# HGRN scores as pairs of 64-column products in the two column halves of the PE array

## The chip, the core and the metric

One Trainium2 chip; the kernel runs on one of its cores. The engines named below are TensorE (PE, with its weight loads as a track of their own, PEld), VectorE (DVE), ScalarE (ACT), GpSimd (POOL) and SyncE (SP, which issues DMAs). The metric is the device time of one execution in microseconds (us), lower is better.

## The reference

One layer of a decoder trunk over 1024 tokens of 1024 features: a normed input projection feeds three mixers (HGRN2, a dilated-window attention, RWKV-7), whose outputs are projected and added to the input; a gated MLP with a short convolution, a gated embedding and a last norm follow. All inputs and outputs are float32. What matters here is HGRN2, with 4 heads of 128 keys and 128 values:

```python
def hgrn2_mix(q_raw, f_raw, i_raw, g_raw, lower_bound, gnorm_g):
    q = jax.nn.silu(q_raw.astype(f32))
    f = lower_bound + (1.0 - lower_bound) * jax.nn.sigmoid(f_raw.astype(f32))
    k = 1.0 - f
...
    def step(state, inp):
        qc, kc, vc, lfc = inp
        b = jnp.cumsum(lfc, axis=2)
        b_last = b[:, :, -1:, :]
        o_inter = jnp.einsum('bhck,bhkv->bhcv', qc * jnp.exp(b), state)
        rel = jnp.where(causal[:, :, None], b[:, :, :, None, :] - b[:, :, None, :, :], -jnp.inf)
        scores = jnp.einsum('bhik,bhjk,bhijk->bhij', qc, kc, jnp.exp(rel))
        o_intra = jnp.einsum('bhij,bhjv->bhiv', scores, vc)
        state = (jnp.exp(b_last[:, :, 0, :])[..., None] * state
                 + jnp.einsum('bhck,bhcv->bhkv', kc * jnp.exp(b_last - b), vc))
        return state, o_inter + o_intra
```

A score of query i and key j is their product over the 128 keys, each weighted by the product of the forget gates between j and i.

## The kernel before, in words

The kernel works in stages. `phase_mix` (line 324) runs the norm, the RWKV-7 mixer together with most of the input projections, and then, interleaved, the four HGRN heads, the window attention and what is left of the projections. `phase_out` projects the mixers' outputs, and the FFN (`phase_up`, `phase_down`) and the embedding follow. All data lie as 128 features by 1024 tokens. Large products are split into three products of rounded float32 parts (`mm3`, line 134).

An HGRN head (`hgrn_head`, line 839) is a Python generator. It takes the sequence in 8 chunks of 128 tokens, held in an order in which the first half of a tile runs backwards; 4 chunks are in each half. Scores of a chunk are a 128 by 128 square, keys by queries, and are built up by levels. The own scores (distance 0, lines 867 to 872) come first: for both halves i, four matmuls of a 128 by 128 key block with a 128 by 128 query block into the PSUM tile `sc`, and a copy through a mask, `copy_predicated`, which writes into S only where the mask is set. Then level l = 1 to 7 (lines 886 to 906) handles pairs of neighbouring blocks of n = 2^(l-1) tokens: keys of one block, queries of the other. `keys(l)` (line 878) gathers the keys on ACT into `ks`; four matmuls (line 891) make `sc`, of which line 893 copies what `mask(l)` selects into S3[0], the first half of S. Lines 894 to 896 multiply gates into one half of the keys `k` (on POOL for odd l, on DVE for even) and of the queries `qt` (on DVE), and line 901 combines the gates of neighbouring blocks for the next level. After level 7 the first half S3[0] holds scores of both sequence halves, and lines 907 and 908 part them: what lies above the diagonal (`mask(8)`) is copied to S3[1] and then set to zero in S3[0]. S3[1] was cleared beforehand by POOL (line 858).

Of every 128 by 128 score square, levels 1 to 6 and the own scores use only the two 64 by 64 squares on the diagonal, level 7 only the two off it. The rest of the product is computed and masked away.

After the levels, values and keys are transposed on PE (`vt`, lines 914 and 920), chunk states are formed (`hkv`, line 935; `hst`, 944) and the outputs follow from scores and states (`hpo`, lines 954 and 956).

The masks are ten 128-column tables in `cst` (lines 54 to 58), loaded once by `load_masks` (line 302) and cast to bytes by POOL; `hgmask(l)` (line 307) picks one.

PSUM: HGRN, the attention and the late projections share four one-bank tiles, tag "mx". The attention uses two tiles of two banks, tag "dp". Around the change work the attention's scores (`swq`, line 1035, 64 rows of the array by 128 columns), its transposes (`swt`, line 1058), its outputs (`swo`, line 1071: 128 rows, 64 columns, one head in each column half) and the projections `zp` (lines 139 to 143 by way of `project_late`).

Two things set the order. `phase_mix` interleaves the generators by a list written out by hand (lines 341 to 344): A is heads 0 and 2, B heads 1 and 3, each handing over after 14 steps, C the attention, F and M projections. From what is so traced, a planner in the build sets the order of instructions on each engine by its own costs of the instructions, and the space of tiles; an engine then executes its queue in that order.

Of the kernel before, what the change touches and what calls it, by code (L numbers as in the profile page):

```python
# [10 lines left out]
F32 = mybir.dt.float32  # L11
# [7 lines left out]
P = 128  # L19
T = 1024  # L20
HT = 512
# [15 lines left out]

CC_ID, CC_BONE, CC_MSK, CC_I64 = 0, 128, 256, 384
NC0 = CC_HG = 448
NCC = CC_HG + 10 * 128  # L40


def shape_constants():
    c = np.zeros((P, NCC), np.float32)
    pp = np.arange(P)[:, None]
    ff = np.arange(P)[None, :]
    c[:, CC_ID:CC_ID + P] = pp == ff
    same = (pp // 64) == (ff // 64)
    c[:, CC_BONE:CC_BONE + P] = same
    f64 = np.arange(64)[None, :]  # L50
    c[:, CC_MSK:CC_MSK + 64] = pp % 64 < f64
    c[:, CC_MSK + 64:CC_MSK + 128] = pp % 64 <= f64
    c[:, CC_I64:CC_I64 + 64] = pp % 64 == f64
    c[:, CC_HG:CC_HG + P] = pp == ff
    for l in range(7):
        n = 1 << l
        c[:, CC_HG + (l + 1) * P:CC_HG + (l + 2) * P] = (pp // n) ^ 1 == ff // n
    c[:, CC_HG + 8 * P:CC_HG + 9 * P] = pp < ff
    u = np.arange(T)[None, :]
    d = pp - (u - 896)  # L60
    cnt = ((d >= 0) & (d <= 128)).astype(np.float64)
    cnt += (d >= 0) & (d <= 512) & (d % 4 == 0)
    cnt += (d >= 0) & (d <= 2048) & (d % 16 == 0)
    sw = np.where(cnt > 0, 8.0 * np.log(np.maximum(cnt, 1.0)), -1e30).astype(np.float32)
    return c, sw
# [26 lines left out]
class Trunk:  # L92
# [183 lines left out]
    def setup(self):  # L276
# [7 lines left out]
        self.id64 = self.cst[:, CC_I64:CC_I64 + 64]  # L284
        self.cmask = cp.tile([P, NCC - NC0], U8, name="cmask")
        few = cp.tile([P, 8], F32, name="few")
# [15 lines left out]
    def load_masks(self, tp):  # L302
        t = tp.tile([P, NCC - NC0], F32, name="ctmp")
        self.nc.gpsimd.dma_start(t, self.a["cst"][:, NC0:])
        self.nc.gpsimd.tensor_copy(self.cmask, t)

    def hgmask(self, l):
        o = CC_HG - NC0 + l * P
        return self.cmask[:, o:o + P]


    def proj(self, j):
# [526 lines left out]
    def hgrn_head(self, h):  # L839
        nc, mxp, par, spool = self.nc, self.mxp, self.par, self.spool  # L840
        j0 = 8 + 4 * h

        def view(t, off, *dims):
            return bass.AP(t.tensor, t.offset + off, [t.ap[0], *dims])

        f = self.zload(j0, self.slot)
        q = self.zload(j0 + 1, self.slot)
        yield
        nc.vector.tensor_scalar(f, f, self.olb[:, h:h + 1], self.lb[:, h:h + 1], ALU.mult, ALU.add)
        k = self.slot("hk")  # L850
        for a, b in ((0, HT), (HT, 0)):
            nc.vector.tensor_scalar(k[:, a:a + HT], f[:, b:b + HT], -1.0, 1.0, ALU.mult, ALU.add)
        qt = self.slot("qt")
# [1 line left out]
        yield  # L855

        S = self.slot("hS")
        nc.gpsimd.memset(S[:, HT:], 0.0)
        S3 = [S[:, a:a + HT].rearrange("p (c i) -> p c i", i=P) for a in (0, HT)]

        def mask(l):
            return self.hgmask(l).unsqueeze(1).broadcast_to([P, 4, P])

        Tt = self.slot("hT")
        off = 0
        Tc = f
        for i in (0, 1):
            sc = mxp.tile([P, 4, P], F32, tag="mx", name=self.nm("hsc"))
            for c in range(4):
                nc.tensor.matmul(sc[:, c, :], k[:, (1 - i) * HT + c * P:(1 - i) * HT + (c + 1) * P],  # L870
                                 q[:, i * HT + c * P:i * HT + (c + 1) * P], start=True, stop=True)
            nc.vector.copy_predicated(S3[i], mask(0), sc)

        def blocks(l):
            n = 1 << (l - 1)
            return n, HT // n, ([HT + n, 2], [2 * n, 256 // n], [1, n])

        def keys(l):
            n, nb, half = blocks(l)
            ks = spool.tile([P, HT], F32, tag="sqt", name=self.nm("ks"), bufs=2)  # L880
            nc.scalar.copy(view(ks, 0, [n, 2], [2 * n, nb // 2], [1, n]), view(k, 0, *half))
            return ks

        ks = keys(1)
        yield
        for l in range(1, 8):
            n, nb, half = blocks(l)
            qq = view(qt, 0, *half)
            sc = mxp.tile([P, 4, P], F32, tag="mx", name=self.nm("hsc"))
            for c in range(4):  # L890
                nc.tensor.matmul(sc[:, c, :], ks[:, c * P:(c + 1) * P],
                                 view(qt, c * P, [2 * n, 64 // n], [HT + n, 2], [1, n]), start=True, stop=True)
            nc.vector.copy_predicated(S3[0], mask(l), sc)
            (nc.gpsimd if l % 2 else nc.vector).tensor_tensor(
                view(k, 0, *half), view(k, 0, *half), view(Tc, nb + 1, [-nb - 1, 2], [2, nb // 2], [0, n]), ALU.mult)
            nc.vector.tensor_tensor(qq, qq, view(Tc, 1, [nb - 1, 2], [2, nb // 2], [0, n]), ALU.mult)
            if l < 7:
                ks = keys(l + 1)
            Tn = Tt[:, off:off + nb]
            T3 = Tc.rearrange("p (b two) -> p b two", two=2)  # L900
            nc.vector.tensor_tensor(Tn, T3[:, :, 0], T3[:, :, 1], ALU.mult)
            Tc = Tn
            off += nb
            if l == 7:
                vc = self.zload(j0 + 2, self.slot)
            yield
        nc.vector.copy_predicated(S3[1], mask(8), S3[0])
        nc.vector.copy_predicated(S3[0], mask(8), self.zero.unsqueeze(1).broadcast_to([P, 4, P]))

        V = self.slot("hV")  # L910
        for hf in (0, 1):
            pt = mxp.tile([P, HT], F32, tag="mx", name=self.nm("vt"))
# [35 lines left out]
        o = self.slot("ho")  # L948
# [710 lines left out]
def lay_out(inp):  # L1659
    f = {k: np.asarray(v) for k, v in inp.items()}  # L1660

    def cols(v):
        return v.reshape(-1, P).T

    lora = np.concatenate([f["rwkv_w2"][0], f["rwkv_a2"][0]], axis=0)
    par = np.concatenate(
        [cols(f["norm_mix_g"][0]), cols(f["norm_ffn_g"][0]), cols(f["norm_ple_g"][0]), cols(f["final_norm_g"]),
         cols(f["hgrn_lower_bounds"][0]), cols(f["hgrn_gnorm_g"][0]), cols(f["rwkv_mu"][0]),
         cols(f["rwkv_w0"][0]), cols(f["rwkv_a0"][0]), cols(f["rwkv_k_k"][0]), cols(f["rwkv_k_a"][0]),
         cols(f["rwkv_r_k"][0].reshape(-1)), cols(f["rwkv_ln_w"][0]), cols(f["rwkv_ln_b"][0]),  # L1670
         cols(f["ffn_conv_w"][0].reshape(-1)), cols(f["ffn_conv_b"][0]), lora, f["rwkv_g2"][0]], axis=1)
    cst, swm = shape_constants()
    return {
        "xT": np.ascontiguousarray(f["x"][0].T).reshape(ND, P, T),
        "pT": np.ascontiguousarray(f["p"][0, 0].T).reshape(2, P, T),
        "w_in": col_blocks(f["w_in"][0], in_blocks()),
        "w_out": col_blocks(f["w_out"][0], range(0, 1024, P)),
        "ffn_up": col_blocks(f["ffn_up"][0], range(0, 5632, P)),
        "ffn_down": np.ascontiguousarray(f["ffn_down"][0]).reshape(NFF, P, 1024),
        "ple_gate": col_blocks(f["ple_gate"][0], range(0, 1024, P)),  # L1680
        "ple_proj": np.ascontiguousarray(f["ple_proj"][0]).reshape(2, P, 1024),
        "par": np.ascontiguousarray(par),
        "cst": cst,
        "swm": swm,
    }
# [17 lines left out]
```

## Time and profile before

| | us |
|---|---|
| median of 3 runs | 1486.92 (1485.7 to 1489.24) |
| profiled execution, its own time | 1488.94 |
| its span | 1487.2 |
| mean granted PE clock | 0.99 |
| HGRN and attention stage, about | 425 to 640 |

A page of the profile tells one execution: busy time of each engine, forty slices of the span, the DMA queues, the chain of work that ended last, and the costliest groups of instructions. Besides the page, the trace answers questions on stretches of time, groups by line and shape, waits and single instructions. L891 is line 891 of the kernel. `128*64 128x128 x8` in a PE row are array rows by array columns used, the moving operand and the count. A float32 matmul stands as two instructions, its two passes. `x28: 684/736/755` are least, median and largest duration in nanoseconds (ns). In a timeline row the first number is the start, the second the length until the last of the merged instructions ended; since matmuls overlap in the pipeline, starts are the better measure.

### The profile page before, as it was taken

To read this page: it belongs to the slowest core of one execution; us is meant where nothing else is said; L and a number is where in the kernel's file an instruction comes from. 1 tells how busy PE (TensorE), PEld (TensorE's weight loads), DVE (VectorE), ACT (ScalarE), POOL (GpSimd) and SP (SyncE) were. 2 spreads that over 40 slices of the span, in tenths; PEclk is the share of its full clock that TensorE was granted. 3 is DMA by queue.
4 is the path that set the end of the run, shared out by engine and by line. 5 is a ranking of instruction groups with operands and counts; after the bars stand their busy time and mean duration, and the time that the engine had idled before them with its cause. 6 is when DMAs were issued, how large, how long until landed. Compare 5 with 4: busy or idle time off the path is not lost.

```text
span 1487.2 us, 22736 instructions
## 1 busy us (share of the span) xinstructions
PE 1437.7 (97%) x8910; PEld 1172.1 (79%) x8910; DVE 1066.6 (72%) x1555; ACT 594.5 (40%) x976; POOL 379.8 (26%) x276
## 2 busy tenths in 40 slices
PE   6999999999999989999999999999999999999996
PEld 5778888788777777878778888888888888888885
DVE  6486243782465788646878888888888799877775
ACT  6522211313124445425454444444444444455552
POOL 2221011200021322122024545444555000002342
PEclk9999999999999999999999999999999999999998
DMA  5124002132061121165223233333332883351353
GB/s 218 43 78 142 31 30 99 51 102 70 30 227 43 65 78 58 44 255 177 106 100 120 99 101 105 106 106 107 106 106 78 305 310 97 103 170 57 114 172 104
DMA packets 79595, 167.90 MB, mean 113 GB/s; under 512 B 19904, under 2 KB 22208, under 8 KB 79488
## 3 DMA queue, kind: packets, MB, share of 16 engines
q1 hardware_dynamic: 66032, 146.39, 29.5%
q10 hardware_dynamic: 12368, 15.99, 3.1%
q0 software_dynamic: 1088, 4.06, 0.8%
q8 instruction: 70, 1.15, 0.3%
q14 instruction: 37, 0.30, 0.1%
HBM read 120.02 MB, written 46.40 MB: 112 GB/s over the span
## 4 chain that ended last, share of the span: by engine, by line
PE 48%; issue 2%; DVE 1%; POOL 1%; DMA 0%; ACT 0%; POOLq 0%; ACTq 0%; DVEq 0%
PE bg L1190 15%; PE bv L1190 12%; PE bv L1484 7%; PE bg L1484 7%; PE bv L139 1%; PE dp L143 1%; PE bv L143 1%; PE bv L141 1%; PE dp L139 1%; PE dp L141 1%; PE bg L139 1%; PE bg L143 1%; PE bg L141 1%; POOL wlo L118 0%; DMA out_dram<-ot 0%
## 5 line engine op out<-in xcount | busy, mean ns | idle before, releaser
L139 PE MATMUL dp<-xh,whi 128*128 128x512 f32 x560 | 193.5, 405 | 9.9 <-ACT xh L380 9.7
L143 PE MATMUL dp<-xh,wlo 128*128 128x512 f32 x560 | 187.0, 394 | 0.8 <-POOL wlo L118 0.8
L141 PE MATMUL dp<-xl,whi 128*128 128x512 f32 x560 | 187.3, 395 | 0.4 <-DVE xl L381 0.3
L118 POOL TENSOR_TENSOR wlo<-wraw,whi 128x512 fp32r<-128x512 f32 x60 | 83.0, 1383 | 314.0 <-ACT whi L116 287.8
L118 POOL TENSOR_TENSOR wlo<-raw,whi 128x512 fp32r<-128x512 f32 x84 | 134.7, 1623 | 76.2 <-ACT whi L116 76.2
L116 ACT CAST whi<-wraw 128x512 fp32r<-128x512 f32 x120 | 73.0, 617 | 167.7 <-PE dp L141 128.4
L1190 PE MATMUL bg<-t,whi 128*128 128x512 f32 x352 | 133.2, 389 | 0.0
L139 PEld LDWEIGHTS dp<-xh,whi 128*128 128x128 f32 x560 | 102.4, 189 | 35.3 <-ACT xh L380 9.7
L141 PEld LDWEIGHTS dp<-xl,whi 128*128 128x128 f32 x560 | 104.8, 189 | 25.6 <-DVE xl L381 2.8
L143 PEld LDWEIGHTS dp<-xh,wlo 128*128 128x128 f32 x560 | 105.5, 189 | 24.3 <-POOL wlo L118 1.2
L118 POOL TENSOR_TENSOR wlo<-s,whi 128x512 fp32r<-128x512 f32 x44 | 63.9, 1452 | 173.7 <-ACT whi L116 160.0
L1484 PE MATMUL bg<-t,whi 128*128 128x512 f32 x308 | 95.1, 390 | 0.0
L1484 PE MATMUL bv<-t,whi 128*128 128x512 f32 x308 | 94.8, 389 | 0.0
L116 ACT CAST whi<-raw 128x512 fp32r<-128x512 f32 x88 | 52.6, 619 | 94.4 <-issue 48.2
L116 ACT CAST whi<-s 128x512 fp32r<-128x512 f32 x66 | 38.9, 620 | 121.0 <-PE bg L1190 113.5
L1190 PEld LDWEIGHTS bg<-t,whi 128*128 128x128 f32 x352 | 66.1, 188 | 13.7
L192 POOL TENSOR_TENSOR rst<-rst,mhalf 128x4 f32<-128x4 f32 (+1 forms) x9 | 10.7, 1192 | 230.2 <-DVE rst L188 214.9
L118 DVE TENSOR_TENSOR wlo<-wraw,whi 128x512 fp32r<-128x512 f32 x60 | 47.4, 792 | 30.1 <-ACT whi L116 25.4
L1484 PEld LDWEIGHTS bv<-t,whi 128*128 128x128 f32 x308 | 57.8, 188 | 11.9
L1190 PE MATMUL bg<-t,wlo 128*128 128x512 f32 x176 | 67.2, 389 | 0.0
L1484 PEld LDWEIGHTS bg<-t,whi 128*128 128x128 f32 x308 | 57.8, 188 | 11.9
L1480 ACT CAST t<-t 128x512 fp32r<-128x512 f32 x77 | 47.8, 621 | 45.7 <-PE bv L1484 31.8
(402 smaller groups left out, 3483.6 us busy)
## 6 DMA issues: line engine op xcount, KB each, us to landing
raw<-in_ffn_up_dram SPq DMA_DIRECT2D x44, 512.0 KB, 3.4
wraw<-in_w_in_dram SPq DMA_DIRECT2D x30, 512.0 KB, 3.5
z<-zst SPq DMA_DIRECT2D x19, 512.0 KB, 3.2
gb<-ct SPq DMA_DIRECT2D x33, 256.0 KB, 2.1
t<-gb SPq DMA_DIRECT2D x33, 256.0 KB, 2.9
t<-gt SPq DMA_DIRECT2D x33, 256.0 KB, 2.7
zl<-z SPq DMA_DIRECT2D x16, 512.0 KB, 4.2
wraw<-in_ple_gate_dram SPq DMA_DIRECT2D x16, 512.0 KB, 3.3
```

Source lines behind the costliest of these rows:

```text
L116: self.cast = nc.scalar.copy(hi, src).ins
L118: eng.tensor_tensor(lo, src, hi.bitcast(F32), ALU.subtract)
L139: nc.tensor.matmul(ps[hf], wh, xh[hf], start=first, stop=False)
L141: nc.tensor.matmul(ps[hf], wh, xl[hf], start=False, stop=False)
L143: nc.tensor.matmul(ps[hf], wl, xh[hf], start=False, stop=last)
L192: nc.gpsimd.tensor_tensor(r2, r, self.mhalf[:, :n], ALU.pow)
L1190: nc.tensor.matmul(ps, w[part == 2][:, s], X[k][part == 1], start=start and k == part == 0, stop=k == 3 and part == 2, skip_group_check=no ...
L1480: nc.scalar.copy(xh, x)
L1484: nc.tensor.matmul(ps[m], wt[part == 2][:, m * P:(m + 1) * P], (xh, xl)[part == 1], start=k == part == 0, stop=k == NK - 1 and part == 2)
```

## The change

The own scores and levels 1 to 6 are computed only in the two diagonal 64 by 64 squares: each matmul becomes two, g = 0 and 64, of 64 keys and 64 queries, with the result in PSUM partitions g to g + 63, so that they use one column half of the PE array each. Masks, score tiles and predicated copies become 64 columns wide. The own scores of both sequence halves go into one PSUM tile; from there they are copied into the left (D) and the right (E) 64 columns of each chunk of S3[0], where the two diagonal squares of a chunk lie one above the other. At level 7 the two products give the two off-diagonal squares without a mask: DVE first parts the levels so far (four copies, 64 partitions each), POOL clears one quarter, and ACT copies the two squares whole. The former parting after level 7 goes. POOL now clears all of S beforehand. The mask table shrinks from 10 x 128 to 12 x 64 columns (9 masks are used).

```diff
-NCC = CC_HG + 10 * 128
+NCC = CC_HG + 12 * 64
...
+    masks = [pp % 64 == f64, *(pp % 64 // n ^ 1 == f64 // n for n in (1, 2, 4, 8, 16, 32)), pp % 64 <= f64, pp % 64 > f64]
...
-        nc.gpsimd.memset(S[:, HT:], 0.0)
+        nc.gpsimd.memset(S, 0.0)
...
+        lo, hi = self.QUADS
+        D = S3[0][:, :, 0:64]
...
+        own = mxp.tile([P, 2, 4, 64], F32, tag="mx", name=self.nm("hsc"))
         for i in (0, 1):
-            sc = mxp.tile([P, 4, P], F32, tag="mx", name=self.nm("hsc"))
             for c in range(4):
-                nc.tensor.matmul(sc[:, c, :], k[:, (1 - i) * HT + c * P:(1 - i) * HT + (c + 1) * P],
-                                 q[:, i * HT + c * P:i * HT + (c + 1) * P], start=True, stop=True)
-            nc.vector.copy_predicated(S3[i], mask(0), sc)
+                for g in (0, 64):
+                    nc.tensor.matmul(own[g:g + 64, i, c, :], k[:, (1 - i) * HT + c * P + g:(1 - i) * HT + c * P + g + 64],
+                                     q[:, i * HT + c * P + g:i * HT + c * P + g + 64], start=True, stop=True)
+        E = S3[0][:, :, 64:128]
+        nc.vector.copy_predicated(D, mask(0), own[:, 1])
+        nc.vector.copy_predicated(E, mask(0), own[:, 0])
...
-            sc = mxp.tile([P, 4, P], F32, tag="mx", name=self.nm("hsc"))
+            sc = mxp.tile([P, 4, 64], F32, tag="mx", name=self.nm("hsc"))
             for c in range(4):
-                nc.tensor.matmul(sc[:, c, :], ks[:, c * P:(c + 1) * P],
-                                 view(qt, c * P, [2 * n, 64 // n], [HT + n, 2], [1, n]), start=True, stop=True)
-            nc.vector.copy_predicated(S3[0], mask(l), sc)
+                for g in (0, 64):
+                    x = view(qt, c * P + g, [2 * n, 32 // n], [HT + n, 2], [1, n]) if l < 7 else \
+                        qt[:, c * P:c * P + 64] if g else qt[:, HT + c * P + 64:HT + (c + 1) * P]
+                    nc.tensor.matmul(sc[g:g + 64, c, :], ks[:, c * P + g:c * P + g + 64], x, start=True, stop=True)
+            if l < 7:
+                nc.vector.copy_predicated(D, mask(l), sc)
+            else:
+                for q, b in ((lo, 0), (hi, 64)):
+                    nc.vector.copy_predicated(S3[1][q, :, b:b + 64], mask(7, q), D[q])
+                nc.vector.copy_predicated(E[hi], mask(8, hi), D[hi])
+                nc.vector.copy_predicated(D[lo], mask(7, lo), E[lo])
+                nc.gpsimd.memset(E[lo], 0.0)
+                nc.scalar.copy(S3[1][lo, :, 64:128], sc[lo])
+                nc.scalar.copy(D[hi], sc[hi])
...
-        nc.vector.copy_predicated(S3[1], mask(8), S3[0])
-        nc.vector.copy_predicated(S3[0], mask(8), self.zero.unsqueeze(1).broadcast_to([P, 4, P]))
```

More of the change, by code (lines that the diff above doesn't have):

```diff
@@ L53, in shape_constants @@
     c[:, CC_I64:CC_I64 + 64] = pp % 64 == f64
[L54 to L58, printed above, removed]
+    masks = [pp % 64 == f64, *(pp % 64 // n ^ 1 == f64 // n for n in (1, 2, 4, 8, 16, 32)), pp % 64 <= f64, pp % 64 > f64]
+    for i, m in enumerate(masks):
+        c[:, CC_HG + i * 64:CC_HG + (i + 1) * 64] = m
     u = np.arange(T)[None, :]
@@ L307, in hgmask @@
     def hgmask(self, l):
-        o = CC_HG - NC0 + l * P
-        return self.cmask[:, o:o + P]
+        return self.cmask[:, l * 64:(l + 1) * 64]
     def proj(self, j):
@@ L857, in hgrn_head, with mask @@
         S = self.slot("hS")
-        nc.gpsimd.memset(S[:, HT:], 0.0)
+        nc.gpsimd.memset(S, 0.0)
         S3 = [S[:, a:a + HT].rearrange("p (c i) -> p c i", i=P) for a in (0, HT)]
-        def mask(l):
-            return self.hgmask(l).unsqueeze(1).broadcast_to([P, 4, P])
+        def mask(l, q=slice(0, P)):
+            return self.hgmask(l)[q].unsqueeze(1).broadcast_to([q.stop - q.start, 4, 64])
+        lo, hi = self.QUADS
+        D = S3[0][:, :, 0:64]
         Tt = self.slot("hT")
```

## The prediction

> **What bounds the kernel now.** I read the page first: the busy shares, then the chain that ended last.
>
> ```profile
> PE 1437.7 (97%) x8910; PEld 1172.1 (79%) x8910; DVE 1066.6 (72%) x1555; ACT 594.5 (40%) x976; POOL 379.8 (26%) x276
> ...
> PE 48%; issue 2%; DVE 1%; POOL 1%; DMA 0%; ACT 0%; POOLq 0%; ACTq 0%; DVEq 0%
> ```
>
> TensorE (PE) is busy 97% of the time, and the chain runs on it. An average says little of one stage, so next I cut the time into stages. The changed code runs inside the first three rows (columns: us, then busy us and instructions of each engine, granted clock, DMA share, GB/s).
>
> ```profile
> 425.00:515.00 90.00, 87.52 (x527) 70.22 (x525) 57.10 (x108) 36.80 (x78) 18.17 (x16) 0.98 0.30 111
> 515.00:608.00 93.00, 84.47 (x644) 65.27 (x643) 75.45 (x143) 47.42 (x101) 24.44 (x20) 0.94 0.18 60
> 608.00:640.00 32.00, 29.33 (x237) 24.93 (x236) 20.02 (x34) 10.86 (x19) 6.53 (x5) 1.00 0.15 50
> 640.00:730.00 90.00, 87.70 (x391) 71.88 (x390) 55.36 (x81) 36.95 (x62) 19.78 (x15) 0.98 0.54 193
> ```
>
> From 425 to 640 PE is busy 201.3 of 215 us, VectorE (DVE) 152.6, ScalarE (ACT) 95.1, POOL 49.1. So PE bounds the stage, and DVE comes second, closest in the second row (75.45 of 93 us, against PE's 84.47). What PE waits for in this stretch, longest first:
>
> ```profile
> PE swt L1058 <- ACT ob L1072: 3.7, 1, 3.7
> PE hsc L891 <- DVE qt L896: 3.3, 6, 1.6
> ```
>
> Of 13.7 idle us, no single cause has more than 3.7. The order is otherwise packed: time taken off PE here should leave the run. Behind the stage PE is again full (87.70 of 90), and the FFN begins its long unbroken chain here:
>
> ```profile
> 747.13 5.23 PE bg L1190 x23
> ```
>
> **Part 1, the score products.** The view of stretches, restricted to the score tile, gives their weight in 425 to 640:
>
> ```profile
> 425.00:640.00 215.00, 42.95 (x288) 37.99 (x288) 26.10 (x36) 0.97 0.23 80
> ```
>
> 288 PE instructions are 36 groups of 8: four matmuls of two passes each; per head seven levels and two groups for the own scores. A group's undisturbed cost, from two neighbours of the same shape:
>
> ```profile
> 480.74 1.05 PE L891 MATMUL hsc<-qt,ks 128*128 128x128 f32 x8
> 481.63 1.95 PE L870 MATMUL hsc<-zl,hk 128*128 128x128 f32 x16
> ```
>
> From 480.74 to 481.63 is 0.89 us: 0.111 a pass. The change makes each matmul two, of 64 stationary and 64 moving columns, so 16 passes a group. What one such pass costs when its partner works in the other half is not in the trace; two rows come near. One is a product that already runs in the two column halves (L1071), with 128 moving columns:
>
> ```profile
> 467.50 0.39 PE L143 MATMUL zp<-xh,wlo 128*128 128x512 f32 x1
> 467.82 0.66 PE L1071 MATMUL swo<-pT,sV 128*64 128x128 f32 x8
> 468.41 0.87 PE L1058 MATMUL swt<-cst,lg 128*128 128x128 f32 x6
> 469.12 1.06 PE L891 MATMUL hsc<-qt,ks 128*128 128x128 f32 x8
> 470.11 1.35 PE L1035 MATMUL swq<-zl,zl 64*128 64x512 f32 x8
> 471.38 0.88 PE L1071 MATMUL swo<-pT,sV 128*64 128x128 f32 x12
> 472.19 1.09 PE L1058 MATMUL swt<-cst,lg 128*128 128x128 f32 x8
> ```
>
> Eight passes take 0.59 us (467.82 to 468.41), twelve 0.81 (471.38 to 472.19): four more for 0.22, or 0.055 each, half of 0.111. So two halves do run side by side. The eight should then take 0.44; the other 0.15 is paid at the change of shape. The other row has 64 moving columns, but in diagonal quarters of the array:
>
> ```profile
> 416.57 1.15 PE L711 MATMUL yt<-cst,y 64*64 64x64 f32 x32
> 417.65 0.70 PE L715 MATMUL pg<-sg,par 128*128 128x512 f32 x1
> ```
>
> 32 passes in 1.08 us; less 0.15 for the change of shape, 0.029 each. I take 0.029: it is the width of the new passes, and half of 0.055 besides. A group then costs 16 x 0.029 = 0.47 instead of 0.89, and 36 groups give back 36 x 0.42 = 15.1 us.
>
> The upper bound is that the two halves cannot load their weights together. A row where the load alone sets the pace, because only two columns move:
>
> ```profile
> L520 PE MATMUL kks<-few,kksq 128*128 128x2 f32 x32 | 3.7, 247 | 0.0
> ```
>
> 3.7 / 32 = 0.116 us for 128 stationary columns, so 0.058 for 64. Loads in turn would make 16 x 0.058 = 0.93 a group: no gain, 36 x 0.04 = 1.4 us lost. Against it stands the weight-load track of the same L1071 group:
>
> ```profile
> 467.82 0.20 PEld L1071 LDWEIGHTS swo<-pT,sV 128*64 128x64 f32 x4 [0.35 <-issue]
> ```
>
> Four loads start and end within 0.20 us; in turn they alone would need 4 x 0.058 = 0.23 before any latency. They overlap. [...]
>
> **Part 2, changes of shape.** Today the groups are full-array like most of their neighbours; tomorrow they are not. I followed all 36 groups in the PE timeline, from 436.33 to 617.14: 18 are entered from a full-array neighbour (new cost), 14 are left into one (new), 6 are left into and 2 entered from half-column products (L1071, L206: a cost that goes), and the rest touch L1035's 64-row products, which change shape either way. An entry costs about 0.15 as above. Leaving into the full array costs more where 128 columns must be loaded unhidden:
>
> ```profile
> 537.42 1.97 PE L1071 MATMUL swo<-pT,sV 128*64 128x128 f32 x32
> 539.32 2.05 PE L870 MATMUL hsc<-zl,hk 128*128 128x128 f32 x16
> 541.21 0.28 PE L891 MATMUL hsc<-qt,ks 128*128 128x128 f32 x1
> ```
>
> 1.90 against 32 x 0.055 = 1.76, and 1.89 against 16 x 0.111 = 1.78: 0.14 + 0.11 = 0.25 at most; I take 0.2. Sum: 18 x 0.15 + 14 x 0.2 - 6 x 0.15 - 2 x 0.2 = +4.2 us (at the least 0, where PE waits at that point anyway).
>
> **Part 3, the predicated copies.** They run on DVE, beside PE.
>
> ```profile
> L893 DVE COPY_PREDICATED hS<-cmask,hsc x28: 684/736/755, 449.0 to 618.3; 128x512 f32<-128x512 uint8 x28
> L872 DVE COPY_PREDICATED hS<-cmask,hsc x8: 700/727/750, 439.9 to 580.0; 128x512 f32<-128x512 uint8 x8
> L858 POOL MEMSET hS<- x4: 517/524/762, 426.1 to 571.6; 128x512 f32 x4
> L907 DVE COPY_PREDICATED hS<-cmask,hS x4: 708/748/1174, 484.6 to 619.5; 128x512 f32<-128x512 uint8 x4
> L908 DVE COPY_PREDICATED hS<-cmask,few x4: 715/740/802, 487.6 to 620.3; 128x512 f32<-128x512 uint8 x4
> ```
>
> Per head 11 copies now: 7 x 0.736 + 2 x 0.727 + 0.748 + 0.740 = 8.1 us. After: 2 own, 6 levels and 4 at the end, 12 of 256 columns. Such a copy is not in the trace; this DVE copy shows what width is worth:
>
> ```profile
> L1059 DVE COPY pT<-swt x16: 240/487/692, 487.4 to 615.0; 128x128 f32<-128x128 f32 x4, 128x256 f32<-128x256 f32 x4, 128x384 f32<-128x384 f32 x4, 128x512 f32<-128x512 f32 x4
> ```
>
> From 128 to 512 columns it grows by 452 ns, 1.18 a column; 736 - 256 x 1.18 = 0.43 (bounds 0.37, half, and 0.736, no gain). I take 0.45: 5.4 a head, 2.7 x 4 = 11 us off DVE (bounds 15 and, at no gain, -3). It counts nothing by itself, being hidden under PE; it matters because PE gains as much, and DVE must not become the later one. 152.6 - 11 = 142 against PE's 201.3 - 10.9 = 190: it does not.
>
> **Part 4, the top level.** ACT gets two copies a head; the nearest row:
>
> ```profile
> L815 ACT COPY y<-pyo x8: 372/381/391, 177.6 to 406.9; 128x256 f32<-128x256 f32 x8
> ```
>
> 8 x 0.38 = 3 us on an engine with 120 idle. The copy into D waits for DVE's copy out of D; queued behind it on ACT are the copies that free PSUM tiles. In the last head ACT has this room:
>
> ```profile
> 620.22 0.27 ACT L1072 COPY ob<-swo 128x128 f32<-128x128 f32 x1 [5.04 <-PE swo L1071]
> ```
>
> POOL clears twice the width of S (0.52 more a head, by the L858 row) and then one quarter of the other half, which waits for DVE. Queued behind that on POOL is the level's key product, which the key transposes on PE need:
>
> ```profile
> 615.32 1.05 POOL L894 TENSOR_TENSOR hk<-hk,hT 128x512 f32<-128x512 f32 x1 [2.56 <-ACT ks L881]
> ```
>
> ```profile
> 621.03 1.04 PE L920 MATMUL vt<-cst,hk 128*128 128x128 f32 x8
> ...
> 624.69 0.83 PE L954 MATMUL hpo<-hV,hS 128*128 128x128 f32 x6
> ```
>
> DVE's four copies (4 x 0.45 = 1.8 us) need only the level before. If they start no earlier than the last L893 copy does now (618.3), they end at 620.1, and clearing and product (0.52 + 1.05) at 621.7, 0.7 late for the 621.03; one level earlier, nothing is late. S itself is read at 624.69, later still. I cost it at nothing, since the copies can go ahead of the level's matmuls; without that cover it is 0.7 a head, 2.8 in all. The own scores take one PSUM tile instead of two, which can only ease waits. The mask table shrinks from 1280 to 768 columns; POOL casts it once, before this idle time, which hides any gain:
>
> ```profile
> 26.92 1.44 POOL L192 TENSOR_TENSOR rst<-rst,mhalf 128x4 f32<-128x4 f32 x1 [8.69 <-DVE rst L188]
> ```
>
> **The sum.** -15.1 + 4.2 + 0 = -10.9 us, all between 425 and 640. The profiled execution took 1488.94 us (span 1487.2), 2.0 above the median of 1486.92; it would become 1478.0, and the median **1476.0**. The remaining uncertainty is the order: a planner sets each engine's order at build from its own costs, which change for every edited instruction. I allow about 5 us either way for it and for waits.
>
> **The rivals.**
>
> A, the halves load in turn. Price from L520: +1.4 on the groups, +4.2 on changes of shape, +5.6: **1492.5**, slower. It decides from 0.048 a pass up (36 x 16 x 0.048 = 27.6, against 36 x 0.89 = 32.0 now less 4.2 for changes of shape). For: no full-height half with 64 moving columns is in the trace. Against: four loads in 0.20 us. [...]
>
> B, PE gets ahead and waits. DVE is at 81% in 515 to 608, its queue is in fixed order, and PE already waits 3.3 us for qt. If the two engines are coupled there, PE's 10.9 is given back as idle time, all but what DVE's and ACT's chains free; with two thirds given back -3.6, about **1483**. The end of each head's top level (2.8 us) belongs here too. For: DVE's 75.45 of 93. Against: DVE gets shorter by as much.
>
> C, the waits shrink too. Half of PE's 13.7 idle us go with the shorter DVE queue, and half of the shape changes fall where PE waits: -10.9 - 6.8 + 2.1 = -15.6, **1471**.
>
> **How the numbers follow.** About 0.2% (3 us) is what a measurement of this kernel can tell from no change. Forecast 0.60 (1471 to 1481), C 0.13, B 0.17 (half of it within 0.2%), A 0.10. Faster 0.60 + 0.13 + 0.08 = 0.81, same 0.09, slower 0.10. The range, from C's end to most of B, is 1467 to 1485: A and the rest of B are left out.
>
> **What would show it.** L891 and L870 become 576 instructions of 128*64 on 64 columns, sixteen starting within about 0.5 us; 0.9 would be A. The score tile's PE time falls from 42.95 to some 27 us, its DVE copies cost about 0.45 each. The row of L1190 at 747.13 moves to about 736, and what follows keeps its length; if it moves less while the groups are short, PE's idle time between 425 and 640 has grown and its releaser says whose queue it was (B). The prediction is wrong if the groups don't halve, or if the order after the change leaves PE idle elsewhere.

## The result and the profile after

The median went from 1487.4 us (1485.7 to 1489.24, 4 runs) to 1475.76 us (1474.41 to 1476.65, 4 runs): ratio 0.9922, with a 95% interval of 0.9909 to 0.9936. The forecast was 1476.0. The profiled execution of after took 1476.02 us (span 1474.2); before's took 1488.94 (span 1487.2).

The first view is the page's busy shares of after. PE is still busy 96% of a span that is 13 us shorter.

```profile
PE 1420.9 (96%) x9198; PEld 1153.4 (78%) x9198; DVE 1053.9 (71%) x1559; ACT 595.8 (40%) x984; POOL 383.1 (26%) x280
```

Two rows of the stages of after follow (columns as in the prediction). In the second, DVE got no lighter against before's 75.45, because the work of the last head moved up into this stretch; PE's share fell to 79.85 of 93 us.

```profile
515.00:608.00 93.00, 79.85 (x876) 61.04 (x878) 77.00 (x159) 51.80 (x112) 22.67 (x21) 0.94 0.20 66
608.00:640.00 32.00, 30.14 (x188) 25.20 (x185) 12.06 (x20) 8.00 (x14) 4.83 (x5) 1.00 0.46 172
```

Fixed windows hold different work before and after, so I cut at landmarks of the program: from the first score product to the transposes that close the last HGRN head (L974 before, L985 after; call this the mixer section), and from there to the first product of the FFN. Before:

```profile
436.33:635.25 198.92, 185.32 (x1327) 147.64 (x1327) 140.48 (x266) 91.18 (x191) 44.91 (x36) 0.97 0.18 62
635.25:742.95 107.70, 105.33 (x469) 86.08 (x469) 69.45 (x103) 45.83 (x75) 21.08 (x16) 0.98 0.52 186
```

After, the same two sections:

```profile
435.88:623.93 188.05, 171.28 (x1616) 130.81 (x1615) 129.52 (x269) 93.00 (x199) 47.74 (x40) 0.97 0.19 65
623.93:730.00 106.07, 103.72 (x469) 84.92 (x469) 69.67 (x103) 45.54 (x75) 20.81 (x16) 1.00 0.52 189
```

The mixer section is 10.87 us shorter (198.92 to 188.05): PE's busy time fell by 14.0 (185.32 to 171.28) and its idle time grew by 3.2 (13.60 to 16.77). The section behind it is 1.6 shorter with the same 469 PE instructions. The row of the chain that marks the FFN moved by 12.9, from 747.13 to 734.22; after it nothing differs.

```profile
734.22 5.23 PE bg L1201 x23
```

Restricted to the score tile, the view of stretches shows where PE's time came from: 25.01 us instead of 42.95, with 576 instructions instead of 288. The DVE column holds the 32 copies out of PSUM, the ACT column the top level's two whole copies a head.

```profile
425.00:640.00 215.00, 25.01 (x576) 20.82 (x576) 13.79 (x32) 2.94 (x8) 0.98 0.27 99
```

What PE waits for in 425 to 640 of after, longest first: the wait for `qt` (3.3 before, now 0.3 by the same view) is gone; waits for `ho` (1.8 before) and for `hS` (none before) are there instead.

```profile
PE swt L1069 <- ACT ob L1083: 4.2, 2, 3.9
PE vt L985 <- DVE ho L979: 4.1, 3, 1.8
PE swd L204 <- DVE hS L875: 2.1, 1, 2.1
PE vt L931 <- ACT hV L926: 1.6, 1, 1.6
```

A term that the prediction had not priced is the granted clock. The sections hold stretches at exactly 0.50, each a multiple of 3.4 us. Before has 3.4 at 439.3, 6.8 at 524.6, 3.4 at 569.0 and 3.4 at 726.0. Two of them:

```profile
524.60:531.40 6.80, 5.71 (x32) 4.65 (x34) 4.40 (x9) 3.75 (x8) 0.00 (x0) 0.50 0.39 142
726.00:729.40 3.40, 3.40 (x10) 2.65 (x9) 3.32 (x6) 0.00 (x0) 0.00 (x0) 0.50 0.12 49
```

After has 6.8 at 518.5 and 3.4 at 559.5, and none in the section behind:

```profile
518.50:525.30 6.80, 6.56 (x51) 5.28 (x51) 3.57 (x9) 3.31 (x9) 0.00 (x0) 0.50 0.33 117
```

Inside these stretches passes of 128x128 start 0.213 us apart instead of 0.111, and of 128x512 0.427 instead of 0.227 (both in before). So a stretch of 3.4 us costs about 1.7 us where PE bounds, an estimate: half of its length. The mixer section lost one (13.6 us at half clock before, 10.2 after), the section behind it one: 1.7 us each. That is the whole 1.6 of the latter.

### The profile page after: what moved, and what is told of

Its sections match the earlier page's. It is cut to its first block, busy times and chain, and to the rows that moved or that the text cites. A ratio compares the mean times of both kernels' runs of the same rounds, so it can differ in the third digit from the quotient of the medians.

```text
span 1474.2 us, 23335 instructions
## 1 busy us (share of the span) xinstructions
PE 1420.9 (96%) x9198; PEld 1153.4 (78%) x9198; DVE 1053.9 (71%) x1559; ACT 595.8 (40%) x984; POOL 383.1 (26%) x280
## 4 chain that ended last, share of the span: by engine, by line
PE 48%; issue 2%; DVE 2%; POOL 1%; DMA 0%; ACT 0%; POOLq 0%; DVEq 0%; ACTq 0%
PE bg L1201 15%; PE bv L1201 12%; PE bv L1495 7%; PE bg L1495 7%; PE bv L137 1%; PE bv L139 1%; PE bv L141 1%; PE bg L137 1%; PE bg L139 1%; PE bg L141 1%; PE dp L137 1%; PE dp L139 1%; PE dp L141 1%; POOL wlo L116 0%; DVE h L1227 0%
## 5 line engine op out<-in xcount | busy, mean ns | idle before, releaser
L1495 PEld LDWEIGHTS bg<-t,whi 128*128 128x128 f32 x308 | 57.8, 188 | 11.9
```

The lines of the kernel that those rows point to most:

```text
L1495: nc.tensor.matmul(ps[m], wt[part == 2][:, m * P:(m + 1) * P], (xh, xl)[part == 1], start=k == part == 0, stop=k == NK - 1 and part == 2)
```

## The experiments

**The theory**: the two halves load and compute side by side, so the score products cost half; the changes of shape cost what the sum says; DVE's relief is hidden. **Its rivals**: the halves work in turn, and the gain is DVE's relief (test 1, 2 and 5 below); the changes of shape cost nothing, or far more (tests 3 and 4); PE loses part of its gain to waits behind other queues (tests 6, 7, 9 and 10). Line numbers are those of after. Differences are of medians, against after's 1475.76.

**1. The halves in turn.** The same products in another order: all four of one half, then all four of the other.

```diff
-            for c in range(4):
-                for g in (0, 64):
+            for g in (0, 64):
+                for c in range(4):
```

> The changed kernel, but within each group all products of the first column half come first and then all of the second, so that neighbouring passes share a half and cannot run side by side. My theory (the gain is the overlap of two halves): a pass then takes 0.055 us instead of 0.029, a group 0.88 instead of 0.47, 36 groups +15 us, so about 1490 to 1491, level with or above the kernel before, although the copies stay narrow. Rival (the gain came from the narrower copies on DVE): it stays within 3 us of 1476.

Measured: 1484.12 us (1481.96 to 1485.76, 8 runs), ratio to before 0.9979 (0.9968 to 0.9989), 8.4 more than after. The queues of DVE, ACT and POOL hold the same instructions in the same order as in after, so this is the array's doing. One group in the PE timeline of after, between the same neighbours as in the experiment:

```profile
462.68 0.49 PE L1069 MATMUL swt<-cst,lg 128*128 128x128 f32 x3
463.10 0.69 PE L897 MATMUL hsc<-qt,ks 128*64 128x64 f32 x16
463.71 0.70 PE L1046 MATMUL swq<-zl,zl 64*128 64x512 f32 x2
```

The same group with the halves in turn:

```profile
464.22 0.97 PE L897 MATMUL hsc<-qt,ks 128*64 128x64 f32 x16
465.11 0.70 PE L1046 MATMUL swq<-zl,zl 64*128 64x512 f32 x2
```

From its start to the neighbour's start a group takes 0.61 us in after and 0.89 in turn: 0.28 more, 10.1 for 36 groups. PE's busy time in the mixer section is 9.0 higher:

```profile
435.60:631.30 195.70, 180.29 (x1615) 139.89 (x1615) 130.58 (x269) 93.06 (x199) 48.30 (x40) 0.96 0.19 63
```

The section is 7.65 longer than after's. It holds 17.1 us at half clock, 6.8 more than after's 10.2, so up to 3.4 of it is clock.

The trace has the start of every single pass. In after they come in pairs: 463.100 and .106, then .206 and .213, .265 and .271, and so on, one pair every 0.058, or 0.029 a pass. In turn they come singly at first, 0.058 apart (464.323, .381, .439), as the prediction's in-turn bound had it. But right after the fifth, at 464.498, another starts at 464.503, then one alone at .556, then pairs at .610 and .668, and single ones again from .727 to .960. Sixteen passes of one half after another would have had no pairs. The sixteen starts fall into two rows of eight with the same steps (one of 0.107, then 0.058 each), one from 464.216 and one from 464.503: the other half's products were begun when five of the first half's eight passes had been. That is read from the start times, since the records don't name the half. So order costs 8.4 us in the run, half-clock time included, and not the 15 that the test forecast from the whole groups' gain.

**2. Twice the copies.** Each predicated copy of levels 1 to 6 is made a second time: 24 more DVE instructions, the same result. (The planner also moved some other instructions in DVE's and ACT's queues.)

```diff
                 nc.vector.copy_predicated(D, mask(l), sc)
+                nc.vector.copy_predicated(D, mask(l), sc)
```

> The changed kernel with the predicated copy of levels 1 to 6 done twice (24 copies more, 24 x 0.444 = 10.7 us on DVE), which gives DVE back about the load it had before. My theory (PE bounds the stage, DVE's saving is hidden): 0 to +4 us, 1476 to 1480. Rival (DVE's saving was half or more of the gain, PE would wait for it otherwise): +6 to +11 us, 1482 to 1487.

Measured: 1481.95 us (1481.84 to 1483.07, 5 runs), ratio 0.9966 (0.9952 to 0.998), 6.2 more than after: the rival's range, not the 0 to 4 of the theory. The mixer section:

```profile
435.50:629.62 194.12, 177.94 (x1624) 135.47 (x1623) 136.72 (x293) 93.42 (x199) 47.16 (x40) 0.95 0.19 63
```

It is 6.07 longer, and yet PE's idle time did not grow (16.2 against 16.8): its busy time grew by 6.7 at the same work. 20.5 us of it were at half clock against 10.2, and half of the difference is 5.1. The largest new stretch follows a pause of PE, 2.1 us idle in 3.0:

```profile
555.00:558.00 3.00, 0.91 (x18) 0.61 (x17) 1.44 (x3) 0.43 (x2) 1.72 (x1) 1.00 0.51 175
558.00:568.20 10.20, 10.07 (x66) 7.52 (x68) 9.74 (x17) 3.91 (x9) 2.38 (x3) 0.50 0.01 2
```

So 10.7 us more of DVE work, about what the change had taken off DVE, gave back half of the change's gain. They added no idle time of PE; they moved its pauses, and more time went by at half clock. That the pauses lower the clock is argued from their order in time (the last section has the count); that most of the time was lost at half clock is shown, and not by this one profile alone: all five runs were granted 0.987 to 0.989 of the clock, where after's four had 0.990 to 0.992.

**3 and 4. A change of shape inside each level.** In the middle of each level's group stands one more product of two moving columns: in test 3 with 128 stationary columns, so that the array changes to its full shape and back; in test 4 with 64, so that it doesn't. Its result is overwritten.

```diff
                     nc.tensor.matmul(sc[g:g + 64, c, :], ks[:, c * P + g:c * P + g + 64], x, start=True, stop=True)
+                if c == 1:
+                    nc.tensor.matmul(sc[:, 3, 0:2], ks[:, 0:P], qt[:, 0:2], start=True, stop=True)
```

(Test 4: `sc[0:64, 3, 0:2], ks[:, 0:64]`.)

> The changed kernel with one more small product in the middle of each of the 28 level groups: 128 by 128 stationary, 2 columns moving, into columns that a later product of the group overwrites. It leaves the half-column shape and comes back, two more changes of shape. Theory (a change of shape costs PE 0.15 to 0.2 us): per group 0.35 for the changes and 0.23 for the two load-bound passes, 28 x 0.58 = +16 us, about 1492. Rival (changes of shape cost nothing that PE doesn't lose anyway): the passes alone, 28 x 0.23 = +6 us, about 1482.

> The control to the run with a full-array product in between: the same small product with 64 stationary columns, so in the shape of its neighbours, with no change of shape. Theory: two passes of 0.058 at most a group, 28 x 0.12 = +3 us, about 1479. If it costs as much as the full-array one (over 1486), the price there is not the change of shape but the interruption of the pairs.

Measured: test 3 1487.61 us (1484.15 to 1492.1, 10 runs), ratio 1.0004 (0.9991 to 1.0017), 11.9 more than after and between the forecasts of theory (1492) and rival (1482); test 4 1479.89 us (1477.59 to 1480.72, 4 runs), ratio 0.9948 (0.9933 to 0.9963), 4.1 more. In test 3 the group splits in the PE timeline:

```profile
464.98 0.45 PE L897 MATMUL hsc<-qt,ks 128*64 128x64 f32 x8
465.36 0.38 PE L899 MATMUL hsc<-qt,ks 128*128 128x2 f32 x2
465.67 0.45 PE L897 MATMUL hsc<-qt,ks 128*64 128x64 f32 x8
466.05 1.13 PE L1048 MATMUL swq<-zl,zl 64*128 64x512 f32 x4
```

It takes 1.07 us instead of 0.61. The score tile's row of test 3:

```profile
425.00:629.00 204.00, 38.39 (x632) 31.42 (x632) 13.82 (x32) 2.93 (x8) 0.97 0.23 79
```

and of test 4, with the same number of instructions:

```profile
425.00:629.00 204.00, 28.86 (x632) 24.43 (x632) 13.81 (x32) 2.93 (x8) 0.97 0.22 79
```

Between the two the tile's PE time differs by 9.5 us, 0.34 in each of the 28 groups. Not all of that is change of shape: the two passes of test 3 load 128 columns and those of test 4 64, by the prediction's figures 0.116 (L520's row) against 0.058 (half of that, an estimate) each. Less that difference the pair of changes (into the full array and back) costs some 0.23 (an estimate), against the 0.15 + 0.2 that the prediction took. The runs lie 7.7 us apart, 0.28 a group: PE's idle time in the mixer section fell from 17.6 (test 4) to 14.6 (test 3) and absorbed part.

**5. No copies.** The other way round from test 2: the kernel leaves out the scores of levels 1 to 6. (Here too the planner moved other instructions.)

```diff
-            if l < 7:
-                nc.vector.copy_predicated(D, mask(l), sc)
-            else:
+            if l == 7:
```

> The changed kernel without the predicated copies of levels 1 to 6 (their scores are left out of the output): 24 x 0.444 = 10.7 us less on DVE, PE's products unchanged. It is the other side of the run with those copies done twice, which cost 6 us, 5 of them as half-clock stretches of PE after its idle time. If DVE's load acts through the queue order (PE idle, then half clock), it may go either way by single stretches of 3.4 us: -5 to +2 us. If PE alone bounds the stage: within 2 us of 1476. If DVE's load counts directly, as much as the doubling: -6 us or more, 1470 or less.

Measured: 1473.87 us (1469.82 to 1475.38, 4 runs), ratio 0.9899 (0.9884 to 0.9913), 1.9 less than after (3.4 by the two ratios; before took 1487.84 beside it). The mixer section:

```profile
435.16:622.00 186.84, 173.38 (x1617) 131.64 (x1616) 123.58 (x245) 93.35 (x199) 47.62 (x40) 0.96 0.19 66
```

The 24 copies left out took 10.6 us; DVE's busy time fell by 5.9 (others of its instructions ran longer, L849 5.8 us in all instead of 3.6, or came into the section), and the section by 1.2. A further relief of DVE as large as the change's own brings at most a third of the change's gain. Tests 1, 2 and 5 together: the array's part is shown by test 1 (8.4 us hang on the order of the products alone, DVE's queue being the same); DVE's relief keeps part of PE's gain from being lost again, most of it as half-clock time, and is not a gain of its own size. The 8.4 of test 1 and the 6.2 of test 2 come to more than the whole 11.6 because both hold half-clock time; the table behind test 10 takes it off.

**6. The attention's values first.** PE's longest wait in after, 3.9 us at 518.7, can be followed back in the timeline:

```profile
514.91 1.21 DVE L851 TENSOR_TENSOR qt<-zl,zl 128x1024 f32<-128x1024 f32 x1
516.04 1.21 DVE L1053 CUSTOM_DVE_ANT_0 lg<-swq,swmask 128x1024 f32<-128x1024 f32 x1
517.30 1.15 ACT L1055 ACTIVATE lg<-lg,sden 128x1024 f32<-128x1024 f32 x1 [7.49 <-DVE sden L1053]
518.45 0.24 ACT L1083 COPY ob<-swo 128x128 f32<-128x128 f32 x1
518.74 0.48 PE L1069 MATMUL swt<-cst,lg 128*128 128x128 f32 x1 [3.94 <-ACT ob L1083]
```

DVE does the gates of the next head before the attention's masking (L1053); ACT stands 7.49 us waiting for that, and behind the waiting instruction in ACT's queue is the copy L1083 which frees PE's PSUM tile. Test 6 issues the products with the values, which end in that copy, ahead of the next scores:

```diff
-                if qb < 8:
-                    cur = self.swa_scores(sp, d, qb)
                 if qb > 1:
                     fin = self.swa_values(sp, d, *pend.pop(0))
+                if qb < 8:
+                    cur = self.swa_scores(sp, d, qb)
```

> A candidate: the changed kernel with the attention's value products and their copy traced ahead of the next block's scores. In the changed kernel PE stood still for 3.9 us near 515 us until ACT had copied the value product out of PSUM, because that copy stood behind an exponential that waited for DVE, and 6.8 us at half clock followed. Theory: the copy goes first, the wait and part of the half clock go, -4 to -7 us, about 1470. Rival (the wait passes to the transposes, which need the exponential anyway, or the new order loses elsewhere): within 2 us of 1476.

Measured: 1477.79 us (1472.53 to 1481.31, 6 runs), ratio 0.9933 (0.9915 to 0.995): no gain, a miss. Its runs were granted 0.985 to 0.991 of the clock, less than after's 0.990 to 0.992. The wait is still there, under another name:

```profile
PE hsc L897 <- ACT pT L1070: 4.3, 2, 4.1
```

What is late is ACT behind DVE, whatever PE does next.

**7. Score groups beside the attention's outputs.** The hand-written order hands over to an HGRN head between the attention's two steps, so that half-column groups should meet half-column neighbours.

```diff
-                order += "C" * (r in self.TURNS) + "A" + "B" * (r > 5) + "F" * (r % 2 and r < 16)
+                order += ("CAC" if r in self.TURNS else "A") + "B" * (r > 5) + "F" * (r % 2 and r < 16)
...
+                yield
                 if 0 < qb < 9:
```

> A candidate: the changed kernel with a step of heads 0 and 2 traced between the attention's value products (also in half-column shape) and its transposes, so that groups come to stand beside a product of their own shape. Theory: up to 22 places save an entry into and an exit out of the shape, 0.3 us each, -6 us at most; if half of the places take effect, -3 us, 1473. Rival (the planner orders by its own costs, and the trace order is not kept; more steps between attention products delay the chain): 0 to +4 us.

Measured: 1476.6 us (1475.97 to 1480.98, 5 runs), ratio 0.9936 (0.9924 to 0.9949): no gain. The planner kept its own order: five groups came to stand behind a `swo` (one in after) and three ahead of one (four in after), so the idea was hardly tried.

**8. After once more**, on the chip of tests 9 and 10, to see how far its time and its half-clock stretches repeat.

> The changed kernel once more, unedited, to see how far its runs spread: other variants gave times in two heaps some 5 us apart. If half-clock stretches of 3.4 us, which cost 1.7 us each, come and go from run to run, the times spread over several us here too; the median stays at 1475 to 1478.

Measured: 1476.32 us (1474.4 to 1478.92, 5 runs), ratio 0.9923 (0.9909 to 0.9938). In its profile the half-clock stretches come again at the same work: 6.8 us at 516.3 and 3.4 at 557.3 (in steps of 10 us the clock is 0.82 and 0.84 from 510 to 530, 0.86 and 0.96 from 550 to 570). So the order of the kernel has a part in them. But they are not the same in every run: the profiled run, of 1474.4 us, was granted 0.992 of the clock, the one of 1478.92 only 0.988.

**9. The head's gates on ACT.** If the wait of test 6 comes from DVE's queue, taking the gates' two scalings from DVE (L846, L849) to the half-idle ACT must help.

```diff
-        nc.vector.tensor_scalar(f, f, self.olb[:, h:h + 1], self.lb[:, h:h + 1], ALU.mult, ALU.add)
+        nc.scalar.activation(f, f, AF.Identity, bias=self.lb[:, h:h + 1], scale=self.olb[:, h:h + 1])
...
-            nc.vector.tensor_scalar(k[:, a:a + HT], f[:, b:b + HT], -1.0, 1.0, ALU.mult, ALU.add)
+            nc.scalar.activation(k[:, a:a + HT], f[:, b:b + HT], AF.Identity, bias=self.ones, scale=-1.0)
```

> A candidate: the changed kernel with the forget gate and the keys of each head computed by ACT instead of DVE (2.2 to 2.7 us a head off DVE, as much on ACT). In the changed kernel these stand in DVE's queue ahead of the attention's reduction at 513 to 516 us, for which ACT and then PE wait. Theory (that queue makes PE's 5 idle us and the 6.8 us at half clock behind them): -3 to -6 us, 1470 to 1473. Rival (PE waits there for the next thing as long, or ACT's added work delays its copies): within 2 us of the changed kernel.

Measured: 1470.86 us (1470.17 to 1472.46, 4 runs), ratio 0.9887 (0.9873 to 0.9901): 5.5 less than test 8 on the same chip. The mixer section:

```profile
434.68:617.04 182.36, 170.71 (x1617) 130.37 (x1617) 125.25 (x263) 98.11 (x205) 47.09 (x40) 0.98 0.20 67
```

DVE gives 4.3 us to ACT, which takes 5.1; PE's busy time is nearly that of after (170.71 against 171.28), and its idle time falls from 16.77 to 11.65. The longest waits of PE now:

```profile
PE vt L985 <- DVE ho L979: 4.0, 3, 1.8
PE swt L1069 <- ACT ob L1083: 3.1, 1, 3.1
```

The wait that it was aimed at lost only 1.1 us of 4.2. The rest came from shorter ones: `hV` (1.6), `sden` (1.2) and `zst` (1.1) no longer appear among PE's waits.

**10. Tests 6 and 9 together.**

> The same with the attention's value products and their copy traced ahead of the next scores. Theory: both remedies act on the same idle time, so together no more than the better one alone: 1470 to 1473. Rival: within 2 us of the changed kernel.

Measured: 1469.79 us (1467.53 to 1472.74, 4 runs), ratio 0.9873 (0.9857 to 0.989). It is the lowest median of all, 6.5 below test 8, but its interval overlaps that of test 9, so the second edit's part in it is not shown.

**The tests at one clock.** Half-clock time blurs every comparison above. The last column takes half of the time in which PE was busy at half clock off the length of the mixer section: an estimate, from one profile each.

| kernel | median against after's | clock granted to its runs | mixer section so reduced, against after's 183.0 |
|---|---|---|---|
| before | +11.6 | 0.990 (profiled run) | +9.6 |
| 1, halves in turn | +8.4 | 0.988 to 0.991 | +5.8 |
| 2, copies twice | +6.2 | 0.987 to 0.989 | +1.9 |
| 3, full array between | +11.9 | 0.986 to 0.992 | +10.2 |
| 4, half array between | +4.1 | 0.988 to 0.992 | +3.7 |
| 5, no copies | -1.9 | 0.989 to 0.993 | -2.5 |
| 6, values first | +2.0 | 0.985 to 0.991 | -1.7 |
| 7, groups beside `swo` | +0.8 | 0.987 to 0.990 | +1.4 |
| 8, after again | +0.6 | 0.988 to 0.992 | +0.7 |
| 9, gates on ACT | -4.9 | 0.991 to 0.992 | -4.1 |
| 10, tests 6 and 9 | -6.0 | 0.989 to 0.993 | -7.0 |

Test 8 shows how far one profile can be trusted: 0.7. The change itself gave some 9.6 us of work and waiting, its order of the halves 5.8 of them, and the doubled copies took only 1.9. Test 6 did shorten the section, by 1.7; the clock took that back.

## Why the prediction was right, point by point

**The groups.** 0.029 a pass and 0.47 a group were right: 32 own passes run from 474.67 to 475.70 in the PE timeline of after, 1.03 us with the exit, and 0.52 for the group before them with part of its entry.

```profile
474.15 0.69 PE L897 MATMUL hsc<-qt,ks 128*64 128x64 f32 x16
474.67 1.10 PE L871 MATMUL hsc<-zl,hk 128*64 128x64 f32 x32
475.70 0.69 PE L1046 MATMUL swq<-zl,zl 64*128 64x512 f32 x2
```

**The changes of shape.** Entry cost 0.14 where 0.15 was taken: in the group at 463.10 the first start comes 0.20 after the last full-array one instead of 0.11, and the second pair 0.106 after the first instead of 0.058. On the way out, the first full-array start comes 0.15 after the last pass instead of 0.03, and the next one 0.16 (`vt`) to 0.21 (`hpo`) after that instead of 0.11: 0.18 to 0.23, where 0.2 was taken. Tests 3 and 4 give some 0.23 for the pair with two moving columns, less than the 0.35. Their sum of 4.2 was probably too high, by the point on the sum below.

**The copies and the top level.** The price of 0.45 a copy was right (0.444):

```profile
L899 DVE COPY_PREDICATED hS<-cmask,hsc x24: 431/444/455, 444.2 to 605.0; 128x256 f32<-128x256 uint8 x24
L902 DVE COPY_PREDICATED hS<-cmask,hS x8: 431/441/1655, 468.5 to 606.6; 64x256 f32<-64x256 uint8 x8
L855 POOL MEMSET hS<- x4: 948/961/1497, 421.1 to 562.3; 128x1024 f32 x4
```

Half as many partitions cost a copy the same (0.441, here out of SBUF), and clearing twice the width 0.44 more a head where 0.52 was taken. In the last head the top level was hidden, as costed, and more safely than the prediction's working had it:

```profile
604.64 1.05 POOL L908 TENSOR_TENSOR hk<-hk,hT 128x512 f32<-128x512 f32 x1 [2.55 <-ACT ks L884]
...
606.17 0.91 DVE L902 COPY_PREDICATED hS<-cmask,hS 64x256 f32<-64x256 uint8 x2
...
607.53 0.37 ACT L907 COPY hS<-hsc 64x256 f32<-64x256 f32 x1
...
607.95 0.31 POOL L905 MEMSET hS<- 64x256 f32 x1 [2.25 <-DVE hS L904]
...
609.70 1.04 PE L931 MATMUL vt<-cst,hk 128*128 128x128 f32 x8
```

POOL's key product (L908) ran at 604.64, ahead of the clearing (607.95) and not behind it, so the queue that the prediction worried about did not form and the transposes at 609.70 wait for nothing.

**The sum.** The mixer section lost 10.87 us where -10.9 was forecast, but not by the forecast's terms alone. PE's busy time fell by 14.0. About 1.3 of that is clock: 12.6 us of it stood at half clock before, 10.0 after. The other 12.7 is work. Counted from each start to the next, with half of the half-clock time taken off, the score products' own time fell by 14.8 (36.7 to 21.9; 15.1 was forecast for the groups) and that of all other products rose by 2.0 (142.4 to 144.4): so the changes of shape, if all the rest is theirs, took back about 2.3 and not 4.2. That term was mis-sized. Against that PE idles 3.2 us longer. The step "the order is otherwise packed: time taken off PE here should leave the run" held only in part; that is rival B, at a quarter of PE's gain instead of two thirds. The FFN came 2 us earlier than the 736 of the prediction, 1.6 of it by the half-clock stretch that before had at 726.0. The total agrees to 0.2 us because a gain larger than forecast and an unpriced gain of clock balance an unpriced wait; the mechanism is shown, that closeness is luck.

**"It counts nothing by itself"**, said of DVE's relief, held for a further relief (test 5, 1.9) but not for the relief that the change brought: with the old load on DVE test 2 lost 6.2, five of them at half clock. The prediction gave the clock no price.

**The rivals.** A is refuted at the width that the prediction could not see: in after passes start in pairs 0.006 apart, their weight loads in pairs 0.007 apart (463.098 and .105, 0.133 us long each), so the loads overlap, and working in turn costs 8.4 more. B came true in part, as above. C did not: the waits changed names and grew.

## What to carry to other kernels

Where half of a product is masked away, two 64-column products in the two column halves can take its place: here a group cost 0.47 us (16 passes at 0.029) instead of 0.89, with the products alternating between the halves (in turn it took 0.28 more) and neighbours of the same shape. A pair of changes of shape (0.23 to 0.37 us here) ate more than half of that gain of 0.42 a group, though only where both neighbours were full. Take what PE gives back only as far as the other queues follow: here the next gain (5.5 us) lay in what DVE did ahead of a step for which ACT waited, and moving that work to ACT got it. When two variants differ by a few us, compare their stretches at half clock, and the clock granted to each run, before explaining the difference by the edit.

## What the runs showed of the hardware

**Half-clock stretches.** All between 430 and 775 us in before and after are one or two times 3.413 us long, at 0.50, each 3.41 costing some 1.7 us where PE is busy (half of it, an estimate). The 10.2 us of test 2 and the 6.8 and 3.4 of test 8 are such multiples too. Within one execution they start on one fixed grid: in before at 439.30, 524.63, 569.00 and 726.02 us, which are 25, 13 and 46 steps of 3.413 us apart, in after at 518.53 and 559.49, 12 apart. The grid lies differently against the program's start in these executions (128.7 steps from the span's start to the first stretch in before, 151.9 in after, 151.3 when it ran again). Counted by the cells of the grid in before and after, the two cells with more than 1.8 us of PE idle time (2.76 in before, 3.41 in after) had half clock behind them, and no stretch began behind a cell with less than 1.20. In between it goes both ways: in before 1.48, 1.63 and 1.20 had one behind them, 1.57 and 1.40 had none; in after the 1.59 before 559.49 had one behind it, the 1.80 at 620.9 had none, and the pause of 2.1 us at 534.3, which a grid point cuts into 1.3 and 0.8, had none. What decides there is open. In tests 2, 8, 9 and 10, PE idled 3.1 to 5.7 of the 10 us from 510 to 520, and the clock was 0.79 to 0.85 there and 0.81 to 0.87 in the next 10. The runs of one kernel in tests 3, 6 and 7 spread over 5 to 9 us, and the granted clock goes with them. In test 3 the run of 1484.15 us was granted 0.992 of the clock, that of 1492.1 us 0.986: shares of 0.008 and 0.014 not granted, or 12 and 21 us, 9 apart where the times are 8 apart.

**Products begun out of order.** In test 1, as read there from the start times, the array began products of the second half (464.503) when three of the first half's eight passes (464.556, .61 and .67) were still to start. By that reading PE did not begin its queue strictly in the planned order.

**DVE beside POOL.** The normalisation L979 took 2.29 us at 509.5 in after, while POOL ran a tensor operation, and 1.23 in the other three heads; behind it L846 took 1.76 instead of 0.81:

```profile
509.52 2.29 DVE L979 TENSOR_TENSOR ho<-ho,hrs 128x1024 f32<-128x1024 f32 x1 [3.23 <-POOL hrs L977]
511.73 1.76 DVE L846 TENSOR_SCALAR zl<-zl,olb,lb 128x1024 f32<-128x1024 f32 x1
```

Before shows the same 2.29 at this place. It is no single case. Between 425 and 640 of after, 16 DVE operations that work on SBUF alone began while POOL ran a tensor operation (0.15 us of overlap or more). Two reductions kept their length; the other 14 took 0.2 to 1.2 us longer, twelve of them by the overlap less 0.12 to 0.14 (L910 1.64 us instead of 0.68 with 1.09 of overlap; for one, L849 at 561.99, POOL's clearing L855 is counted in). Together that is 12.6 us of DVE's time, more than the 11.0 that the change took off DVE in the mixer section. Eleven that began before POOL's operation kept theirs, and so did 29 with an operand in PSUM, the copies L899 and the masking L1053 among them (at most 0.04 longer). The two shown stand in DVE's queue just ahead of the wait that test 6 followed, and made it later by up to 2.0 us.
